# Delta rule decay exponents: one fp32 product against two float32r products

## The chip, the cores and the metric

The kernel is one program on one of the eight cores of a Trainium2 chip. The metric is the device time of one execution in microseconds. A core has TensorE (PE, matrix products; its weight loads are told apart as PEld), VectorE (DVE), ScalarE (ACT), GpSimd (POOL) and SyncE (SP), which issues most of the transfers. Each works through a queue of its own in the order in which the program was built; semaphores make one engine wait for another. Nothing is reordered on the chip, so that an instruction that waits holds up all that is queued behind it on its engine.

## What is computed

Two transformer blocks run one after the other on 256 tokens of width 1024, everything in fp32 to the outside. The first is attention, cross attention to a memory and a feed-forward part. The change lies in the second, a hybrid layer: one projection of the normalized input gives the inputs of a gated delta rule (8 heads), of a sparse attention with an indexer, and of two sigmoid gates that mix the two results; then come an output projection and a feed-forward part.

```
proj = rms_norm(x) @ w_in             # split into g_qkv, g_z, g_a, g_b, a_q, ..., gate_a, gate_b
g = -exp(a_log) * softplus(g_a + dt_bias)            # log decay, 8 heads
o_gdn = gated_delta_rule_chunked(gq, gk, gv, g, beta)
o_att = dsa_sparse_attention(...)
x = x + (sigmoid(gate_a) * norm(o_gdn) * silu(z) + sigmoid(gate_b) * o_att) @ w_out
x = x + square(relu(rms_norm(x) @ w_mlp_up)) @ w_mlp_down

# inside the delta rule, chunk by chunk:
g_cum = cumsum(g)
diff  = g_cum[:, None] - g_cum[None, :]
decay = where(incl, exp(diff), 0)                    # incl: lower triangle with diagonal
a_mat = where(strict, (k * beta) @ k.T * decay, 0)
u, w  = triangular_solve(I + a_mat, ...)
qk    = where(incl, q @ k.T * decay, 0)
```

The change is in how `diff` is formed. The kernel works in two chunks of 128 tokens. For each chunk and head it needs the 128x128 matrix of the sums of `g` from one token to another, and takes its exponential.

## The kernel before, in words

**Matrix products.** Nearly all large products are done in three float32r passes. A weight tile arrives as `raw` (128x1024 fp32), ScalarE casts it to its high half `whi`, and VectorE subtracts to get the low half `wlo`. The activations are split in the same way into `xhi` and `xlo` while they are transposed. `mm3` (line 233) then issues high x high, high x low and low x high into one PSUM bank. Small products with exact needs are fp32, and one fp32 product is two records in the trace.

**Emission.** The order of every queue is fixed when the program is built. The large products (the main stream) are emitted one after the other. After each third pass the builder calls `tick` (line 261), which lets side chains advance: generators such as `chain_gates`, `chain_decay`, the attention `dsa`, the delta rule `gdn`, and the gating at the end. A chain yields what it waits for, and `tick` resumes it once the builder's own running estimate of the engines' times (a fixed part and a rate for each engine, lines 113 to 120; `mm`, line 211, for TensorE) says that it is ready and that ScalarE and VectorE are not too far behind. `pump` (line 316) emits the next weight splits whenever a weight unit has been used. `finish` (line 272) drives given chains to their end. So each instruction that is emitted moves the estimate, and a later choice may come out another way.

**Around the change.** `consts2` (line 1060) builds the constants of block 2 in the course of block 1, among them `strict`, the strictly triangular matrix of zeros and ones; `tri` is the other triangle. `chain_gates` (line 1174) makes the log decays `gg` (128 x 2 chunks x 8 heads). `chain_decay(b)` (line 1338) runs for two halves of the heads and two chunks each: VectorE multiplies `tri` by the columns of `gg` into `gt` (four heads side by side, 128x512), TensorE adds up `strict` times `gt` and, with `identb` and `umb` in bf16, a large negative number above the diagonal, and ScalarE writes the exponential of the bank `ep` into `QE`. `chain_u` waits for it. Its results go into the triangular inverse (whose blocks are merged through `T` and `xp`), and further into the delta rule.

**The end of block 2.** The main stream ends with the products of the two gates: `gn`, for one gate, `gs` for its second half. Beside them run the last chains: attention scores, softmax rows `p`, their transposes on TensorE (`tb<-ident,p`, line 225), attention products `ao`, division by the row sums (`oat`), gating (`Z`), and the transposes of `Z` (`tb<-ident,Z`) whose split halves `xhi`, `xlo` are the input of the output projection, again `gs` products. `k.finish(*s_ga[0])` (line 1778) stands between gate and output projection. Then come a norm (`xg`) and the feed-forward part.

Of the kernel before, what the change touches and what calls it, by code (L numbers as in the profile page):

```python
# [9 lines left out]
F32 = mybir.dt.float32  # L10
F32R = mybir.dt.float32r
BF16 = mybir.dt.bfloat16
AF = mybir.ActivationFunctionType
OP = mybir.AluOpType
AX = mybir.AxisListType

P = 128
# [10 lines left out]
def bcast_rows(ap, n, parts=P):  # L28
    return bass.AP(tensor=ap.tensor, offset=ap.offset, ap=[[0, parts], [1, n]])


def rows(src, r0, nkt, c0, nc_):

    n = src.shape[1]
    return bass.AP(tensor=src.tensor, offset=src.offset + r0 * n + c0,
                   ap=[[n, P], [P * n, nkt], [1, nc_]])
# [6 lines left out]
def flat(ap):  # L43
    return ap.rearrange("p a b -> p (a b)")


def bc(ap, n):

    return ap[:, :, None].to_broadcast([P, ap.shape[1], n])


def mid(ap, n):

    return ap[:, None, :].to_broadcast([P, n, ap.shape[1]])
# [291 lines left out]
def split(k, hi, lo, src, scale=None):  # L346
    nc = k.nc
    if scale is None:
        nc.scalar.copy(hi, src)
        nc.vector.tensor_tensor(lo, src, hi.bitcast(F32), op=OP.subtract)  # L350
    else:
        nc.scalar.activation(hi, src, AF.Copy, scale=scale)
        nc.vector.scalar_tensor_tensor(lo, src, scale, hi.bitcast(F32), op0=OP.mult, op1=OP.subtract)
# [305 lines left out]
def join(sides):  # L659

    if sides:
        yield list(sides)
# [397 lines left out]
def consts2(k, w_in, conv_t, a_log, dt_bias, gdn_norm_g, q_norm_g, k_norm_g, rope_tab):  # L1060

    nc = k.nc
    dma = nc.sync.dma_start

    yield 30.0
    raw = k.t4([P, KT, 88], name="w88")
    dma(raw[:, :, 0:16], rows(w_in, 0, KT, C_AB, 16))
    yield 8.0
    dma(raw[:, :, 16:88], rows(w_in, 0, KT, C_IK, 72))
    yield 12.0  # L1070
    k.rt = k.keep([P, 2, 96], "rt")
    dma(k.rt, rope_tab.rearrange("(h p) c -> p h c", p=P))
    k.cw = k.keep([P, 24, 4], "cw")
    yield 8.0
    dma(k.cw, conv_t)
    yield 5.0
    k.dtb, k.nal = k.keep([P, 8], "dtb"), k.keep([P, 8], "nal")
    dma(k.dtb, bcast_rows(dt_bias, 8))
    dma(k.nal, bcast_rows(a_log, 8))
    yield 5.0  # L1080
    qkg = k.t2([P, 2, P], name="qkg")
    dma(qkg[:, 0], bcast_rows(q_norm_g, P))
    dma(qkg[:, 1], bcast_rows(k_norm_g, P))
    yield 5.0
    k.gng = k.keep([P, P], "gng")
    dma(k.gng, bcast_rows(gdn_norm_g, P))
    yield raw, k.gng
    k.w88 = k.t4([P, KT, 88], F32R, "w88h"), k.t4([P, KT, 88], F32R, "w88l")
    split(k, k.w88[0], k.w88[1], raw)
    yield qkg  # L1090

    k.rg = [k.keep([P, 2, 64], f"rg{i}") for i in range(2)]
    for i in range(2):
        for h in range(2):
            g = qkg[:, i]
            nc.vector.tensor_tensor(k.rg[i][:, h, 0:32], k.rt[:, h, 0:32], g[:, 0:32], op=OP.mult)
            nc.vector.tensor_tensor(k.rg[i][:, h, 32:48], k.rt[:, h, 32:48], g[:, 16:32], op=OP.mult)
            nc.vector.tensor_tensor(k.rg[i][:, h, 48:64], k.rt[:, h, 48:64], g[:, 0:16], op=OP.mult)
    k.gqk = k.keep([P, P], "gqk")
    nc.vector.memset(k.gqk[:, 0:32], 1.0)  # L1100
    nc.vector.tensor_tensor(k.gqk[:, 32:], qkg[:, 0, 32:], qkg[:, 1, 32:], op=OP.mult)

    k.strict = k.keep([P, P], "strict")
    nc.gpsimd.affine_select(k.strict, k.ones, pattern=[[-1, P]], compare_op=OP.is_gt, fill=0.0,
                            base=0, channel_multiplier=1)
    um = k.t2([P, P], name="um")
    nc.gpsimd.memset(um, 0.0)
    nc.gpsimd.affine_select(um, um, pattern=[[1, P]], compare_op=OP.is_ge, fill=NEG,
                            base=0, channel_multiplier=-1)
    k.umb = k.keep([P, P], "umb", BF16)  # L1110
    nc.gpsimd.tensor_copy(k.umb, um)

    k.bm = k.keep([P, 4], "bm")
    nc.gpsimd.affine_select(k.bm, k.ones[:, :4], pattern=[[-32, 4]], compare_op=OP.is_ge, fill=0.0,
                            base=0, channel_multiplier=1)
    nc.gpsimd.affine_select(k.bm, k.bm, pattern=[[32, 4]], compare_op=OP.is_gt, fill=0.0,
                            base=32, channel_multiplier=-1)

    k.bt = k.keep([P, 2], "bt")
    nc.gpsimd.tensor_tensor(k.bt[:, 0:1], k.bm[:, 0:1], k.bm[:, 2:3], op=OP.add)  # L1120
    nc.gpsimd.tensor_copy(k.bt[:, 1:2], k.bm[:, 1:2])
# [18 lines left out]
def block2(k, x3, ht, st, out, conv_w, norm_mlp_g):  # L1140
    nc = k.nc
# [27 lines left out]
    s_small = k.add(chain_small())  # L1169


    gx, ge, gg, beta, iw = (k.keep([P, 2, 8], n) for n in ("gx", "ge", "gg", "beta", "iw"))

    def chain_gates():
        yield from join([s_small])
        yield sml
        nc.vector.tensor_tensor(gx, sml[:, :, 0:8], mid(k.dtb, 2), op=OP.add)
        nc.scalar.activation(beta, sml[:, :, 8:16], AF.Exp, scale=-1.0)
        nc.vector.scalar_tensor_tensor(ge, gx, -1.0, gx, op0=OP.mult, op1=OP.min)
        nc.scalar.activation(ge, ge, AF.Exp)  # L1180
        nc.scalar.activation(k.nal, k.nal, AF.Exp)
        nc.scalar.activation(ge, ge, AF.Ln, bias=1.0)
        yield ge
        nc.vector.scalar_tensor_tensor(gx, gx, 0.0, ge, op0=OP.max, op1=OP.add)
        nc.vector.scalar_tensor_tensor(gg, gx, -1.0, mid(k.nal, 2), op0=OP.mult, op1=OP.mult)
        nc.vector.tensor_scalar(beta, beta, 1.0, None, op0=OP.add)
        nc.vector.reciprocal(beta, beta)
    s_gates = k.add(chain_gates())


# [129 lines left out]
    tri = k.tri1[:, :P]  # L1320
# [17 lines left out]
    def chain_decay(b):  # L1338

        yield from join([s_gates])  # L1340
        yield gg
        for ch in range(2):
            gt = k.t2([P, 4, P], name="gt")
            nc.vector.tensor_tensor(gt, mid(tri, 4), bc(gg[:, ch, 4 * b:4 * b + 4], P), op=OP.mult)
            yield gt
            ep = yield from k.get((P, 4, P), "ep")
            k.mm(flat(ep), k.strict, flat(gt), True, False)
            k.mm(ep, k.identb, mid(k.umb, 4), False, True)
            yield ep
            nc.scalar.activation(QE[ch][:, 4 * b:4 * b + 4], ep, AF.Exp)  # L1350
            k.put()
# [33 lines left out]

    s_dec = k.add(chain_dec())
    s_decay = [k.add(chain_decay(b)) for b in range(2)]
    s_u = []
    gemm_t(k, ht, D, conv_evac(kc, 8, lambda b, sides: s_u.append(k.add(chain_u(b, sides), rank=0))))
# [416 lines left out]
@with_exitstack  # L1806
def tile_kernel(ctx, tc, x, mem, w_in, b_fgt, rel, g_fox_out, g_chk_out, w_out, g_mix_pre, g_mix_post,
                g_mem_kv, w_mq, w_mk, w_mv, w_mo, g_mem_pre, g_mem_post, w_ff1, w_ff2, g_ff_pre, g_ff_post,
                norm_mix_g_2, w_in_2, conv_t, a_log_2, dt_bias_2, gdn_norm_g_2, q_norm_g_2, k_norm_g_2,
                w_out_2, norm_mlp_g_2, w_mlp_up_2, w_mlp_down_2, rope_tab, out):  # L1810
    k = Kern(ctx, tc)
    ctx.enter_context(tc.manual_schedule())
    k.units = units1(w_in, w_mk, w_mv, w_out, w_mq, w_mo, w_ff1, w_ff2)
    k.units += units2(w_in_2, w_out_2, w_mlp_up_2, w_mlp_down_2)
    box = []

    def xt_next():
        if not box:
            box.append(XT(k))
        return box[0]  # L1820
    x3, st = block1(k, x, mem, w_in, b_fgt, rel, g_fox_out, g_chk_out, w_out, g_mix_pre, g_mix_post,
                    g_mem_kv, w_mq, w_mk, w_mv, w_mo, g_mem_pre, g_mem_post, w_ff1, w_ff2, g_ff_pre, g_ff_post,
                    norm_mix_g_2, xt_next,
                    lambda: k.add(consts2(k, w_in_2, conv_t, a_log_2, dt_bias_2, gdn_norm_g_2, q_norm_g_2,
                                          k_norm_g_2, rope_tab)))
    block2(k, x3, box[0], st, out, conv_t, norm_mlp_g_2)
    k.finish()
# [53 lines left out]
```

## Time and profile before

| | |
|---|---|
| three runs | 885.59, 886.88 and 889.85 us; median 886.88 |
| the profiled execution | 885.71 us, span 883.7 |
| TensorE busy | 873.8 us, 99% of the span, 5704 matmul records |
| VectorE busy | 589.5 us, 67% |
| ScalarE busy | 455.2 us, 52% |
| GpSimd busy | 90.0 us, 10% |

A timeline row gives the start of an instruction or of a group of like ones, its duration, the engine, the line, out<-in, the size, and in brackets how long the engine had been idle before it and whose result it waited for. Line 96 is the helper through which all instructions of ScalarE, VectorE and GpSimd pass, line 212 the helper for products and 225 that for transposes; so work is told apart by the names of its tiles. Records of matrix products overlap, since they are pipelined: two rows at 0.23 us distance can each show 0.39 us.

### The profile page before, as it was taken

How to read it: one execution, taken by the hardware profiler on the slowest of the kernel's cores; microseconds unless marked ns; L12 is line 12 of the kernel's file. 1: busy time of each engine (PE TensorE's matmuls, PEld its weight loads, DVE VectorE, ACT ScalarE, POOL GpSimd, SP SyncE). 2: the span in 40 equal slices, each digit the busy share in tenths (PEclk: the TensorE clock that was granted, in tenths of full speed). 3: DMA queues.
4: the chain of work that ended last, by engine and by line, in shares of the span. 5: the costliest groups of instructions: out<-in, count | busy, mean ns of one | idle time of the engine just before them, and what ended most of it. 6: DMA issues, size and time to landing. Idle time of an engine off the chain costs nothing.

```text
span 883.7 us, 14576 instructions
## 1 busy us (share of the span) xinstructions
PE 873.8 (99%) x5704; PEld 774.7 (88%) x5704; DVE 589.5 (67%) x1028; ACT 455.2 (52%) x779; POOL 90.0 (10%) x150
## 2 busy tenths in 40 slices
PE   8999999999999999999999999999999999999998
PEld 7979998899789999998798899988987889999997
DVE  5675665765687556554769999979578875555541
ACT  6674654554475444442656665554564654444440
POOL 3101010100020000000100038800010000000000
PEclk9999999999999999999999999999999999999999
DMA  8992437383377766654651677395125586666521
GB/s 266 293 253 73 144 121 254 104 263 112 90 245 223 203 197 183 189 187 154 172 152 49 191 173 199 82 251 168 49 74 193 179 247 211 192 187 185 195 80 48
DMA packets 162615, 150.86 MB, mean 171 GB/s; under 512 B 20082, under 2 KB 127218, under 8 KB 162547
## 3 DMA queue, kind: packets, MB, share of 16 engines
q1 hardware_dynamic: 161970, 148.88, 56.6%
q10 hardware_dynamic: 576, 1.05, 0.4%
q8 instruction: 45, 0.74, 0.3%
q14 instruction: 24, 0.19, 0.1%
HBM read 148.08 MB, written 1.84 MB: 170 GB/s over the span
## 4 chain that ended last, share of the span: by engine, by line
PE 92%; DVE 4%; ACT 3%; issue 0%; DMA 0%; POOL 0%; DVEq 0%; ACTq 0%; POOLq 0%
PE gt L212 33%; PE acc L212 20%; PE gs L212 13%; PE gn L212 11%; PE tb L225 3%; PE mo L212 3%; DVE wlo L96 1%; PE o L212 1%; ACT p L96 1%; ACT whi L96 1%; PE ops L212 1%; PE ms L212 1%; PE s L212 1%; ACT junk L96 1%; DVE Z L96 1%; PE qp L212 1%
## 5 line engine op out<-in xcount | busy, mean ns | idle before, releaser
L96 DVE TENSOR_TENSOR wlo<-raw,whi 128x1024 fp32r<-128x1024 f32 (+1 forms) x263 | 315.1, 1225 | 111.8 <-ACT whi L96 110.2
L96 ACT CAST whi<-raw 128x1024 fp32r<-128x1024 f32 (+1 forms) x264 | 268.1, 1047 | 85.7 <-DMA raw<-in_w_in_dram 32.3
L212 PE MATMUL gt<-xhi,whi 128*128 128x256 f32 x832 | 239.0, 287 | 0.0
L212 PE MATMUL gt<-xlo,whi 128*128 128x256 f32 x832 | 233.7, 281 | 0.0
L212 PE MATMUL gt<-xhi,wlo 128*128 128x256 f32 x832 | 233.4, 281 | 0.0
L212 PEld LDWEIGHTS gt<-xhi,whi 128*128 128x128 f32 x832 | 156.9, 189 | 1.9 <-issue 1.3
L212 PEld LDWEIGHTS gt<-xlo,whi 128*128 128x128 f32 x832 | 156.9, 189 | 0.6
L212 PEld LDWEIGHTS gt<-xhi,wlo 128*128 128x128 f32 x832 | 156.9, 189 | 0.0
L212 PE MATMUL acc<-whi,ul 128*128 128x512 f32 (+1 forms) x288 | 106.1, 369 | 0.0
L212 PE MATMUL acc<-wlo,uh 128*128 128x512 f32 (+1 forms) x288 | 106.1, 369 | 0.0
L212 PE MATMUL acc<-whi,uh 128*128 128x512 f32 (+1 forms) x288 | 106.1, 368 | 0.0
L212 PE MATMUL gs<-whi,xhi 128*128 128x512 f32 (+1 forms) x208 | 80.6, 388 | 0.5 <-ACT xhi L96 0.5
L212 PE MATMUL gs<-whi,xlo 128*128 128x512 f32 (+1 forms) x208 | 79.1, 380 | 0.3 <-DVE xlo L96 0.3
L212 PE MATMUL gs<-wlo,xhi 128*128 128x512 f32 (+1 forms) x208 | 78.8, 379 | 0.1
L212 PE MATMUL gn<-whi,xhi 128*128 128x512 f32 x160 | 67.3, 420 | 0.0
L212 PE MATMUL gn<-whi,xlo 128*128 128x512 f32 x160 | 63.0, 394 | 0.0
L212 PE MATMUL gn<-wlo,xhi 128*128 128x512 f32 x160 | 62.8, 393 | 0.0
L212 PEld LDWEIGHTS acc<-whi,ul 128*128 128x128 f32 x288 | 54.1, 188 | 9.7
L212 PEld LDWEIGHTS acc<-whi,uh 128*128 128x128 f32 x288 | 54.1, 188 | 9.6
L212 PEld LDWEIGHTS acc<-wlo,uh 128*128 128x128 f32 x288 | 54.2, 188 | 9.5
L96 DVE TENSOR_TENSOR r<-r 128x512 f32<-128x512 f32 x32 | 22.1, 690 | 59.9 <-ACT r L96 59.9
L96 ACT ACTIVATE r<-gt 128x512 f32<-128x512 f32 x24 | 14.3, 598 | 76.1 <-PE gt L212 76.1
(364 smaller groups left out, 1129.2 us busy)
## 6 DMA issues: line engine op xcount, KB each, us to landing
raw<-in_w_in_dram SPq DMA_DIRECT2D x84, 512.0 KB, 4.8
raw<-in_w_ff_dram SPq DMA_DIRECT2D x64, 512.0 KB, 4.7
raw<-in_w_mlp_up_dram SPq DMA_DIRECT2D x32, 512.0 KB, 5.8
raw<-in_w_mlp_down_dram SPq DMA_DIRECT2D x32, 512.0 KB, 4.4
raw<-in_w_out_dram SPq DMA_DIRECT2D x16, 512.0 KB, 4.1
raw<-in_w_mk_dram SPq DMA_DIRECT2D x8, 512.0 KB, 4.1
raw<-in_w_mv_dram SPq DMA_DIRECT2D x8, 512.0 KB, 4.1
raw<-in_w_mq_dram SPq DMA_DIRECT2D x8, 512.0 KB, 4.5
```

The costliest lines, as they stand in the source:

```text
L96: f(*args, **kw)
L212: self.nc.tensor.matmul(out, lhsT, rhs, start=start, stop=stop)
L225: self.nc.tensor.transpose(out, in_, self.ident[:n, :n])
```

## The change

The log decays `gg` are split into a high part `ggh`, rounded to float32r by a ScalarE copy, and the rest `ggl`, subtracted on VectorE. Matrices of both are made: the high one, `gth`, on ScalarE as four scaled copies of `tri` of 128x128, the low one, `gtl`, on VectorE in the place of `gt`. Since `strict` holds only zeros and ones, its copy `strictr` in float32r is exact, and two float32r passes take the place of the fp32 product. The chain now waits for `ggl` where it waited for `gg`, and for `gth` and `gtl` where it waited for `gt`.

```
--- before.py
+++ after.py
@@ -1103,6 +1103,8 @@
     k.strict = k.keep([P, P], "strict")
     nc.gpsimd.affine_select(k.strict, k.ones, pattern=[[-1, P]], compare_op=OP.is_gt, fill=0.0,
                             base=0, channel_multiplier=1)
+    k.strictr = k.keep([P, P], "strictr", F32R)
+    nc.scalar.copy(k.strictr, k.strict)
     um = k.t2([P, P], name="um")
     nc.gpsimd.memset(um, 0.0)
     nc.gpsimd.affine_select(um, um, pattern=[[1, P]], compare_op=OP.is_ge, fill=NEG,
@@ -1169,7 +1171,8 @@
     s_small = k.add(chain_small())
 
 
-    gx, ge, gg, beta, iw = (k.keep([P, 2, 8], n) for n in ("gx", "ge", "gg", "beta", "iw"))
+    gx, ge, gg, beta, iw, ggl = (k.keep([P, 2, 8], n) for n in ("gx", "ge", "gg", "beta", "iw", "ggl"))
+    ggh = k.keep([P, 2, 8], "ggh", F32R)
 
     def chain_gates():
         yield from join([s_small])
@@ -1183,8 +1186,10 @@
         yield ge
         nc.vector.scalar_tensor_tensor(gx, gx, 0.0, ge, op0=OP.max, op1=OP.add)
         nc.vector.scalar_tensor_tensor(gg, gx, -1.0, mid(k.nal, 2), op0=OP.mult, op1=OP.mult)
+        nc.scalar.copy(ggh, gg)
         nc.vector.tensor_scalar(beta, beta, 1.0, None, op0=OP.add)
         nc.vector.reciprocal(beta, beta)
+        nc.vector.tensor_tensor(ggl, gg, ggh.bitcast(F32), op=OP.subtract)
     s_gates = k.add(chain_gates())
 
 
@@ -1338,13 +1343,17 @@
     def chain_decay(b):
 
         yield from join([s_gates])
-        yield gg
+        yield ggl
         for ch in range(2):
-            gt = k.t2([P, 4, P], name="gt")
-            nc.vector.tensor_tensor(gt, mid(tri, 4), bc(gg[:, ch, 4 * b:4 * b + 4], P), op=OP.mult)
-            yield gt
+
+            gh, gl = (k.t2([P, 4, P], F32R, n) for n in ("gth", "gtl"))
+            for j in range(4):
+                nc.scalar.activation(gh[:, j], tri, AF.Copy, scale=ggh[:, ch, 4 * b + j:4 * b + j + 1].bitcast(F32))
+            nc.vector.tensor_tensor(gl, mid(tri, 4), bc(ggl[:, ch, 4 * b:4 * b + 4], P), op=OP.mult)
+            yield gh, gl
             ep = yield from k.get((P, 4, P), "ep")
-            k.mm(flat(ep), k.strict, flat(gt), True, False)
+            k.mm(flat(ep), k.strictr, flat(gh), True, False)
+            k.mm(flat(ep), k.strictr, flat(gl), False, False)
             k.mm(ep, k.identb, mid(k.umb, 4), False, True)
             yield ep
             nc.scalar.activation(QE[ch][:, 4 * b:4 * b + 4], ep, AF.Exp)
```

TensorE's queue gets `ep<-gth,strictr` and `ep<-gtl,strictr` where `ep<-gt,strict` stood, four times; apart from that, all engines issue the same work as before. But the new instructions move the builder's estimate, and from the beginning of `chain_gates` to the start of the feed-forward part many of them stand in another place. Three places follow, each the difference of the two orders: - is the row before, + the row now.

VectorE, after the last softmax scaling `nmx`: `Z` here is the attention-free part of the merged tile, scaled by head (four products of 128x128 for each half of the tokens), `wlo` a weight split.

```order
 L96 TENSOR_TENSOR nmx<-mx,nasc 128x2
-L96 TENSOR_TENSOR t_7026<-t_7026,r_7025 128x4
-L96 SCALAR_TENSOR_TENSOR Z<-qs__6855,t_7026,Z 128x128 x4
-L96 TENSOR_TENSOR wlo<-raw,whi 128x1024
-L96 TENSOR_TENSOR t_7063<-t_7063,r_7062 128x4
-L96 SCALAR_TENSOR_TENSOR Z<-qs__6857,t_7063,Z 128x128 x4
-L96 TENSOR_TENSOR wlo<-raw,whi 128x1024
+L96 TENSOR_TENSOR wlo<-raw,whi 128x1024
+L96 TENSOR_TENSOR t_7077<-t_7077,r_7076 128x4
+L96 SCALAR_TENSOR_TENSOR Z<-qs__6895,t_7077,Z 128x128 x4
+L96 TENSOR_TENSOR t_7095<-t_7095,r_7094 128x4
+L96 SCALAR_TENSOR_TENSOR Z<-qs__6897,t_7095,Z 128x128 x4
```

One split that stood between and one that stood behind the two groups of `Z` are gone there, and one now stands ahead of both. The other stands further up, ahead of the scores.

VectorE, where the gate has been applied and the output projection begins: `Z<-gt__7183` and its successor are the third merged tile, `xlo` the low half of the transposed tiles.

```order
-L96 SCALAR_TENSOR_TENSOR Z<-gt__7183,Z 128x512
+L96 SCALAR_TENSOR_TENSOR Z<-gt__7205,Z 128x512
 L96 TENSOR_TENSOR Z<-Z,oat 128x512
-L96 TENSOR_TENSOR wlo<-raw,whi 128x1024 x2
-L96 SCALAR_TENSOR_TENSOR xlo<-tb,xhi 128x4x128
-L96 TENSOR_TENSOR wlo<-raw,whi 128x1024
+L96 TENSOR_TENSOR wlo<-raw,whi 128x1024 x3
 L96 SCALAR_TENSOR_TENSOR xlo<-tb,xhi 128x4x128 x2
 L96 TENSOR_TENSOR wlo<-raw,whi 128x1024 x4
```

Three weight splits now stand in a row ahead of the first `xlo`, where two stood; the fourth stands behind two `xlo`.

TensorE at the end of the gate product: `tb` are transposes of merged tiles, the `gs` rows ahead of them belong to the gate product, those behind them to the output projection.

```order
 L212 MATMUL gs<-wlo,xhi 128x512
 L212 MATMUL gs<-whi,xlo 128x512
-L212 MATMUL gs<-whi,xhi 128x512
-L212 MATMUL gs<-wlo,xhi 128x512
-L212 MATMUL gs<-whi,xlo 128x512
+L225 MATMUL tb<-ident,Z 128x128 x8
 L212 MATMUL gs<-whi,xhi 128x512
 L212 MATMUL gs<-wlo,xhi 128x512
```

Before, the gate product had the transposes of the first tile nine products ahead of its end, those of the second three ahead, and those of the third at its end. Now those of the first and the third stand together at its end, and those of the second follow three products of the output projection later.

Counted in the whole orders, in products of 512 columns: the last-but-one group of `ao` was followed by 15 gate products, three transposes of `p`, and 9 more gate products up to the last `ao`; it is now followed by 18, the transposes, and 6. Behind the last `ao` stood 45 products of the gate, now 30. The whole attention group stands 15 products later against the main stream, the merge products `xp` 12 products earlier, and the transposes of the second norm 12 products earlier.

## Rows read from the trace of the kernel before

**Rows 1.** Page, first part: each engine's busy us, share of the span, instructions.
```profile
PE 873.8 (99%) x5704; PEld 774.7 (88%) x5704; DVE 589.5 (67%) x1028; ACT 455.2 (52%) x779; POOL 90.0 (10%) x150
```

**Rows 2.** Waits of TensorE: engine, operation, producer waited for; us in total, times, longest.
```profile
PE tb L225 <- ACT p L96: 0.8, 4, 0.3
...
PE gs L212 <- ACT xhi L96: 0.5, 2, 0.3
...
PE gs L212 <- DVE xlo L96: 0.3, 1, 0.3
```

**Rows 3.** Timeline of PE, 653 to 662: start us, us, instruction, count, [idle before].
```profile
655.34 0.48 PE L212 MATMUL gn<-whi,xhi 128*128 128x512 f32 x1
655.66 0.39 PE L212 MATMUL gn<-wlo,xhi 128*128 128x512 f32 x1
655.89 0.40 PE L212 MATMUL gn<-whi,xlo 128*128 128x512 f32 x1
```

**Rows 4.** Timeline of PE, 672 to 677: output projection begins.
```profile
674.32 0.39 PE L212 MATMUL gs<-wlo,xhi 128*128 128x512 f32 x1
675.05 0.50 PE L212 MATMUL gs<-whi,xlo 128*128 128x512 f32 x1 [0.35 <-DVE xlo L96]
```

**Rows 5.** Timeline of PE, 460 to 480: the decay exponents.
```profile
468.54 1.12 PE L212 MATMUL ep<-gt,strict 128*128 128x512 f32 x2
469.50 0.38 PE L212 MATMUL ep<-umb,identb 128*128 128x512 bf16 x1
469.71 1.02 PE L212 MATMUL ep<-gt,strict 128*128 128x512 f32 x2
470.57 0.38 PE L212 MATMUL ep<-umb,identb 128*128 128x512 bf16 x1
```

**Rows 6.** Timeline of ACT, 455 to 481: a scaled copy of 256 columns.
```profile
460.44 0.84 ACT L96 ACTIVATE cy<-gt,cw 128x256 f32<-128x256 f32 x2 [1.55 <-PE gt L212]
```

**Rows 7.** Windows: stretch, its us, busy us of PE, PEld, DVE, ACT, POOL; clock, DMA.
```profile
460.00:480.00 20.00, 20.00 (x149) 16.20 (x148) 19.02 (x56) 13.86 (x29) 0.00 (x0) 1.00 0.19 54
```

**Rows 8.** Timeline of PE, 600 to 675: transposes of the softmax rows.
```profile
618.25 0.49 PE L225 MATMUL tb<-ident,p 128*128 128x128 f32 x3
...
647.11 0.29 PE L225 MATMUL tb<-ident,p 128*128 128x128 f32 x1
647.66 0.44 PE L225 MATMUL tb<-ident,p 128*128 128x128 f32 x2 [0.26 <-ACT p L96]
```

**Rows 9.** Timeline of DVE, 655 to 675: the chain to the output projection.
```profile
657.83 0.16 DVE L96 TENSOR_TENSOR nmx<-mx,nasc 128x2 f32<-128x2 f32 x1
...
661.38 0.15 DVE L96 TENSOR_TENSOR t<-t,r 128x4 f32<-128x4 f32 x1
...
662.75 1.23 DVE L96 TENSOR_TENSOR wlo<-raw,whi 128x1024 fp32r<-128x1024 f32 x1
663.90 0.17 DVE L96 RECIPROCAL ars<-asum 128x4 f32<-128x4 f32 x1
...
671.43 0.69 DVE L96 TENSOR_TENSOR Z<-Z,oat 128x512 f32<-128x512 f32 x1
672.04 2.35 DVE L96 TENSOR_TENSOR wlo<-raw,whi 128x1024 fp32r<-128x1024 f32 x2
674.31 0.68 DVE L96 SCALAR_TENSOR_TENSOR xlo<-tb,xhi 128x512 fp32r<-128x512 f32 x1
```

**Rows 10.** Timeline of ACT, 655 to 662: between scores and gate.
```profile
658.09 0.49 ACT L96 ACTIVATE p<-lg,nmx,asc 128x128 f32<-128x128 f32 x1 [1.53 <-DVE t L96]
...
659.17 1.03 ACT L96 CAST whi<-raw 128x1024 fp32r<-128x1024 f32 x1
660.10 0.59 ACT L96 ACTIVATE gt__7123<-gn 128x512 f32<-128x512 f32 x1
```

**Rows 11.** Tile T: operations, duration ns min/median/max, first and last start.
```profile
L212 PE MATMUL xp<-T,U x96: 190/191/267, 598.4 to 610.0; 32*32 32x32 f32 x64, 64*64 64x64 f32 x32
...
L96 ACT ACTIVATE T<-tpk,bt x2: 732/748/764, 590.1 to 590.7; 128x512 f32<-128x512 f32 x2
```

More of the change, by code (lines that the diff above doesn't have):

```diff
@@ L1105, in consts2 @@
                             base=0, channel_multiplier=1)
+    k.strictr = k.keep([P, P], "strictr", F32R)
+    nc.scalar.copy(k.strictr, k.strict)
     um = k.t2([P, P], name="um")
@@ L1169, in block2 @@
     s_small = k.add(chain_small())
-    gx, ge, gg, beta, iw = (k.keep([P, 2, 8], n) for n in ("gx", "ge", "gg", "beta", "iw"))
+    gx, ge, gg, beta, iw, ggl = (k.keep([P, 2, 8], n) for n in ("gx", "ge", "gg", "beta", "iw", "ggl"))
+    ggh = k.keep([P, 2, 8], "ggh", F32R)
     def chain_gates():
@@ L1185, in chain_gates @@
         nc.vector.scalar_tensor_tensor(gg, gx, -1.0, mid(k.nal, 2), op0=OP.mult, op1=OP.mult)
+        nc.scalar.copy(ggh, gg)
         nc.vector.tensor_scalar(beta, beta, 1.0, None, op0=OP.add)
         nc.vector.reciprocal(beta, beta)
+        nc.vector.tensor_tensor(ggl, gg, ggh.bitcast(F32), op=OP.subtract)
     s_gates = k.add(chain_gates())
@@ L1340, in chain_decay @@
         yield from join([s_gates])
-        yield gg
+        yield ggl
         for ch in range(2):
-            gt = k.t2([P, 4, P], name="gt")
-            nc.vector.tensor_tensor(gt, mid(tri, 4), bc(gg[:, ch, 4 * b:4 * b + 4], P), op=OP.mult)
-            yield gt
+            gh, gl = (k.t2([P, 4, P], F32R, n) for n in ("gth", "gtl"))
+            for j in range(4):
+                nc.scalar.activation(gh[:, j], tri, AF.Copy, scale=ggh[:, ch, 4 * b + j:4 * b + j + 1].bitcast(F32))
+            nc.vector.tensor_tensor(gl, mid(tri, 4), bc(ggl[:, ch, 4 * b:4 * b + 4], P), op=OP.mult)
+            yield gh, gl
             ep = yield from k.get((P, 4, P), "ep")
-            k.mm(flat(ep), k.strict, flat(gt), True, False)
+            k.mm(flat(ep), k.strictr, flat(gh), True, False)
+            k.mm(flat(ep), k.strictr, flat(gl), False, False)
             k.mm(ep, k.identb, mid(k.umb, 4), False, True)
```

## The prediction

> **What bounds the kernel now.** I read the page's first part, then the list of what TensorE waited for, then timelines of single engines at the two places where the new program differs in a way that could matter. TensorE is busy 99% of the span [rows 1], and its waits on a named producer in the second block are tiny: 0.8 us in four waits for the softmax rows `p`, 0.5 in two for the activations' high half `xhi`, 0.3 for one low half `xlo` [rows 2]. A busy matmul record overlaps its neighbour, so I take the pace from start to start. In an undisturbed run of gate products the starts stand 0.23 us apart (655.66 to 655.89), the one after a switch from fp32 takes 0.32 [rows 3]. So the kernel is TensorE's queue, one product after the other, and an edit counts if it changes what that queue holds or makes it stand still. The second is possible where a long dependent chain (attention, delta rule, gating, output projection) must end before the queue can go on. The last such place is around 675 us: the first output product with `xlo` starts at 675.05, 0.73 us after its predecessor, where 0.23 is the pace [rows 4].
>
> **The products themselves.** The change touches four fp32 products `ep<-gt,strict`, each two records. Read start to start in [rows 5], the first takes 0.96 us (468.54 to 469.50), the second 0.86 (469.71 to 470.57); the other two read like the second, so 0.96 + 3 x 0.86 = 3.5 us. In their place come eight float32r products of 128x512. No float32r product on `strictr` is in the trace; the nearest rows are the gate products, float32r of the same width, at 0.23 us: 8 x 0.23 = 1.8 us. Gain 1.7 us. The other end is that a pass costs what an fp32 record costs, 0.43 us: 8 x 0.43 = 3.5, gain nothing. I take 1.7, the row of the same type and width. The Trainium skill (TensorE: Matmul & The Clock Gate, "Back-to-back issue gap") gives about 131 ns for a 512-column product in a stream of loads and products; this trace does not agree, its row says 230 ns. By the page the gain would be about 2.5 us, an estimate from that page.
>
> **ScalarE and VectorE around them.** ScalarE gets sixteen 128x128 scaled copies, and three small casts. The nearest row is a scaled copy of 256 columns, two in 0.84 us [rows 6], so one copy costs between half of 0.42 and all of it: 3.4 to 6.7 us in sum. ScalarE is busy 13.9 of 20 us between 460 and 480 and TensorE does not stand still there [rows 7], and the copies are issued some 45 products of 256 columns ahead of the first `ep`: I cost them at nothing. If that cover is gone, the excess over the 6.1 idle us stalls TensorE, 0.6 us at most. VectorE makes the four low matrices in place of four of the same size, and one 16-column subtraction: it stays at 19 of 20 us busy, and loses below 0.2 us. That is hidden too, since TensorE does not wait for a weight split here. `strictr` is one copy, far ahead in block 1: nothing.
>
> **The order.** The builder lets side chains run by its own running estimate of engine times, and the new instructions shift every decision after 460 us. Counted in the whole orders of before and of the change, the last-but-one group of attention products (`ao`, which ends at 655.34 when the gate product `gn` resumes [rows 3]) now stands 15 products of 512 columns later in TensorE's queue: 15 x 0.23 = 3.5 us. All that comes before it is otherwise the same work. Ahead of it two waits of TensorE inside the transposes of `p` should go: a group of three takes 0.49 us undisturbed, 0.99 at 647.11 and about as much in the group after it [rows 8], 1.0 us too much in sum; they have six more gate products between scores and transposes now. So that point comes at 3.5 - 1.7 - 1.0 = +0.8 us. The bounds: 0.8 if both gains come, 3.5 if neither.
>
> From that point on TensorE has less left to do before it must have the merged activations. The last `ao` used to be followed by 45 gate products, now by 30. The chain from 655.34 is VectorE's, and its length doesn't shrink with that. Before: softmax scaling `nmx` at 657.83, attention output scaled from 663.90, third merged tile `Z` done at 672.12 (671.43 + 0.69), two weight splits `wlo` until 674.31, `xlo` until 674.99 [rows 9], and TensorE at 675.05 [rows 4]: 19.7 us. Now: after `nmx` (+2.65) ScalarE does `p`, a gate tanh and the cast `whi`; these take 1.08 (658.09 to 659.17), 0.5 and 0.95 us [rows 10], so +5.2; the split `wlo`, 1.13, now stands ahead of the `Z` products, then two groups of four products with their small scaling, 1.37 each (661.38 to 662.75), which gives +9.1 where it was 8.56. The third `Z` follows 8.2 us later as before (663.90 to 672.12), +17.3. Then three splits stand ahead of `xlo` instead of two: 3 x 1.13 = 3.4, so `xlo` begins at +20.7 and ends at +21.4, against 19.65: 1.7 us more. `nmx` itself may come 0.7 earlier, since one split less stands ahead of it while the chain waits; I take +1.2, with 0.3 (the splits find idle time) and 3.4 (all three add) as ends.
>
> TensorE meets this at two spots. The transposes of the first and the third `Z` now stand together, right behind the gate product; the second of them waits about 2 us for its `Z`. Then the third output product waits about 3 us for `xlo`. Before, the same stretch held 0.5 us. After the output projection the block's second norm has its transposes 12 products earlier than before, but one split less ahead of them on VectorE, so I cost it at nothing; if it isn't covered, below 1 us. The rest (feed-forward) is the same order.
>
> **Sum:** 3.5 (15 products moved ahead) - 1.7 (passes) - 1.0 (waits gone) + 1.2 (longer chain) = +2.0 us. The profiled execution took 885.71 us, so 887.7. It lies 1.2 us below the median of the three runs, 886.88; from the median it would be 888.9. I forecast 888.2, between. With all lower ends the sum is 3.5 - 1.7 - 1.0 + 0.3 = +1.1, with all upper ends 3.5 + 3.4 = +6.9.
>
> **Rivals.** (1) The chain is no limit, TensorE's shorter queue shows in full: 885.7 - 1.7 - 1.0 = 883.0. For it: 99% busy, waits of 1.6 us in the list [rows 1, 2]. Against it: in [rows 4, 9] the chain ended right at TensorE's need, and it now starts later in the queue; it needs `Z` and `xlo` some 4 us sooner than my count. The Trainium skill (Perfetto Trace Analysis, "Identifying Performance Opportunities") says that a kernel generally improves with its most-contended engine, which here is TensorE; that would be this rival, and the trace bears it out for the long gemm stretches only.
> (2) Slower than 0.5%: a new wait further up, at the merge of the inverse blocks. Its first product `xp` starts at 598.4 and its input `T` is written from 590.1 on, by 591.5 [rows 11]. In the new queue it stands 12 products earlier, 2.8 us, and the passes give 1.7: TensorE comes at 593.9, with 2.4 us of slack left instead of 6.9. `T` hangs on GpSimd and two DMAs, which don't get faster with TensorE. If `T` comes more than 2.4 us later relative to now, TensorE stands still for the excess, and it decides once it eats the 2.7 us of gains: 885.7 + 3.5 + 1.2 = 890.4, and 1:1 more beyond. Against it: the products that feed `T` stand 9 earlier too.
> (3) The change doesn't do what it says: a float32r pass on these operands is no faster than an fp32 record. The order moves all the same: +3.7, 889.4.
>
> **How the numbers follow.** Forecast 0.62 (886.8 to 890), rival 1 0.18, rival 2 0.13, rival 3 0.07. About 0.5% (4.4 us) is what a measurement of this kernel can tell from no change. Faster than 882.4 only rival 1 with luck in the runs reaches: 0.06. Slower than 891.3 needs rival 2 with a large wait or the upper ends together: 0.12. Same 0.82. The range goes from 883.0 (rival 1) to 891.5 (the lower part of rival 2, and the scatter of the runs).
>
> **What would show it.** Right: `ep` products at about 0.23 us start to start; no wait inside the transposes of `p` before the last `ao`; a wait of TensorE of some 2 us before a `tb<-Z` and of some 3 before a `gs` product with `xlo`, where three `wlo` precede `xlo` on VectorE; the first output product with `xlo` at about 677. Wrong: these two waits below 1 us in sum, or a wait before `xp` or `ep`, or `ep` at 0.43.

## The result

| | before | changed |
|---|---|---|
| median of the runs | 887.05 us (6 runs, 885.59 to 889.91) | 894.80 us (6 runs, 893.66 to 894.96) |
| ratio | | 1.0084, 95% interval 1.0069 to 1.0098 |
| profiled execution, span | 885.71, 883.7 us | 894.82, 893.1 us |

The change makes the kernel 0.84% slower, 7.8 us between the medians and 9.1 us between the two profiled executions. The prediction was 888.2 us with 883.0 to 891.5 around it: the sign of its sum was right, the size was not, and the time lies outside the range.

### The profile page after: what moved, and what is told of

Its sections match the earlier page's. It is cut to its first block, busy times and chain, and to the rows that moved or that the text cites. A ratio compares the mean times of both kernels' runs of the same rounds, so it can differ in the third digit from the quotient of the medians.

```text
span 893.1 us, 14596 instructions
## 1 busy us (share of the span) xinstructions
PE 876.6 (98%) x5704; PEld 775.4 (87%) x5704; DVE 590.9 (66%) x1029; ACT 461.1 (52%) x797; POOL 88.7 (10%) x150
## 4 chain that ended last, share of the span: by engine, by line
PE 90%; DVE 5%; ACT 4%; issue 1%; DMA 0%; POOL 0%; DVEq 0%; ACTq 0%; POOLq 0%
PE gt L212 32%; PE acc L212 20%; PE gs L212 13%; PE gn L212 11%; PE tb L225 3%; PE mo L212 3%; DVE wlo L96 2%; PE o L212 1%; ACT p L96 1%; ACT whi L96 1%; DVE Z L96 1%; PE ops L212 1%; PE ms L212 1%; PE s L212 1%; ACT junk L96 1%
```

## The profile after

First the page: the busy times, which answer to [rows 1], and the clock granted to TensorE in 40 slices.

```profile
PE 876.6 (98%) x5704; PEld 775.4 (87%) x5704; DVE 590.9 (66%) x1029; ACT 461.1 (52%) x797; POOL 88.7 (10%) x150
...
PEclk9999999999999999999999999999997999999999
```

TensorE is busy 2.8 us longer with the same 5704 records, and stands still 6.6 us more (the span is 9.4 longer). In one slice (670 to 692 us) the clock is below 9 tenths. Then TensorE's waits (us in total, times, longest), which answer to [rows 2].

```profile
PE tb L225 <- DVE Z L96: 3.0, 2, 2.0
PE gs L212 <- DVE xlo L96: 2.0, 1, 2.0
PE s L212 <- DVE oat L96: 0.8, 1, 0.8
PE ao L212 <- ACT pt L96: 0.8, 1, 0.8
...
PE tb L225 <- ACT p L96: 0.4, 2, 0.3
```

Five of the 9 us stand in the first two lines, where before there were 0.3 us in sum. The waits for `oat` and `pt` are new as well; of the transposes of `p` 0.4 us are left of 0.8 (0.2 of each lie in block 1).

The products of the change themselves, one of four pairs in TensorE's timeline (start us, us, instruction), answer to [rows 5].

```profile
471.02 0.58 PE L212 MATMUL ep<-gth,strictr 128*128 128x512 f32 x1
471.44 0.40 PE L212 MATMUL ep<-gtl,strictr 128*128 128x512 f32 x1
471.68 0.39 PE L212 MATMUL ep<-umb,identb 128*128 128x512 bf16 x1
```

This pair and its switch take 0.66 us (471.02 to 471.68), where the fp32 product took 0.86; the others take 0.56, 0.47 and 0.66. Over all four it is 2.36 us instead of 3.54, 1.2 us gained.

Next the point which the prediction calls the last-but-one `ao` group; it answers to [rows 3].

```profile
659.47 0.94 PE L212 MATMUL ao<-kv,pt 128*128 128x128 f32 x6 [0.75 <-ACT pt L96]
660.16 0.48 PE L212 MATMUL gn<-whi,xhi 128*128 128x512 f32 x1
```

It ends at 660.16, where it was 655.34: 4.8 us later, of which 0.3 us lie ahead of all changes (from 276 to 455 us the second program runs 0.3 us behind the first). TensorE's timeline from there to the output projection answers to [rows 4].

```profile
673.55 0.40 PE L212 MATMUL gs<-whi,xlo 128*128 128x512 f32 x1
674.93 0.66 PE L225 MATMUL tb<-ident,Z 128*128 128x128 f32 x4 [0.99 <-DVE Z L96]
677.59 1.11 PE L225 MATMUL tb<-ident,Z 128*128 128x128 f32 x4 [2.00 <-DVE Z L96]
...
681.60 0.79 PE L212 MATMUL gs<-whi,xlo 128*128 128x512 f32 x1 [2.04 <-DVE xlo L96]
682.19 1.05 PE L225 MATMUL tb<-ident,Z 128*128 128x128 f32 x4
682.90 0.77 PE L212 MATMUL gs<-whi,xhi 128*128 128x512 f32 x1
683.47 0.63 PE L212 MATMUL gs<-wlo,xhi 128*128 128x512 f32 x1
683.90 0.63 PE L212 MATMUL gs<-whi,xlo 128*128 128x512 f32 x1
...
686.75 0.39 PE L212 MATMUL gs<-whi,xhi 128*128 128x512 f32 x1
```

The last pass of the gate product starts at 673.55, TensorE waits 1.0 us for the first `Z` and 2.0 us for the third, then 2.0 us for `xlo`. What follows, from 682.90 on, are the same products as before, but 0.43 us apart in place of 0.23 (683.47 to 683.90), until 686.75. VectorE in the same stretch, as in [rows 9]:

```profile
662.77 0.16 DVE L96 TENSOR_TENSOR nmx<-mx,nasc 128x2 f32<-128x2 f32 x1
...
676.85 0.69 DVE L96 TENSOR_TENSOR Z<-Z,oat 128x512 f32<-128x512 f32 x1
677.46 3.49 DVE L96 TENSOR_TENSOR wlo<-raw,whi 128x1024 fp32r<-128x1024 f32 x3
680.86 1.29 DVE L96 SCALAR_TENSOR_TENSOR xlo<-tb,xhi 128x512 fp32r<-128x512 f32 x2
```

Three `wlo` stand from 677.46 to 680.86, and `xlo` after them. Last the windows of that stretch: us, busy us of PE, PEld, DVE, ACT, POOL, granted clock, DMA share, GB/s.

```profile
673.80:675.00 1.20, 0.21 (x2) 0.07 (x2) 1.17 (x3) 0.60 (x1) 0.00 (x0) 1.00 0.00 0
...
676.00:677.00 1.00, 0.00 (x0) 0.00 (x0) 0.97 (x3) 0.23 (x1) 0.00 (x0) 0.67 0.00 0
...
682.00:686.00 4.00, 4.00 (x12) 3.17 (x12) 2.50 (x3) 1.87 (x2) 0.00 (x0) 0.50 0.89 286
...
687.00:690.00 3.00, 3.00 (x15) 2.44 (x14) 2.30 (x4) 1.55 (x3) 0.00 (x0) 1.00 1.02 378
```

The clock is full in the first stretch, falls while TensorE stands still in the second, and is at a half (1.2 of 2.4 GHz) over the four microseconds from 682 to 686, in which TensorE is busy without a break. At 687 it is full again. The Trainium skill (TensorE: Matmul & The Clock Gate, "What's actually happening") says that the array runs at half its clock after it has stood idle, and comes back to the full one only after it has been busy for a while; the rows agree: 0.67 at 676 to 677, where no product runs, 0.50 at 682 to 686, with PE busy 4.00 of 4.00, and 1.00 at 687.

So the 9.3 us at 686.75 (the tenth product behind the one that waited for `xlo`, 677.47 before) are: 0.3 from ahead of the change, 4.5 until the `ao` group, 1.7 more in the chain from there (660.16 to 681.60 is 21.4 us, 655.34 to 675.05 was 19.7), 2.3 of products at half the clock (681.60 to 686.75 is 5.15 us; ten products at 0.23 and four transposes with their switches, 0.54, make 2.85), and 0.45 for the second tile's transposes, which used to stand ahead of the wait.

## The experiments

Two theories. **Order:** the time went into where instructions now stand (TensorE reaches the output projection with too little left to do, waits, and loses its clock). **Arithmetic:** the added copies, matrices or float32r passes themselves cost it. Times of the kernel before are those of the same chip and session, 886.4 to 886.7 us. TensorE's 5704 records stand in one order in the kernel before and e1, in one in the changed kernel and e2, and in one in e10 and e13.

**e1: the changed arithmetic in the old order.** The new instructions are issued without the builder's estimate being told of them (`eng` is the engine itself, behind the helper of line 96 that keeps the estimate; the gates' two instructions and `strictr` go the same way):

```
-        nc.scalar.copy(ggh, gg)
+        nc.scalar.eng.copy(ggh, gg)
-                nc.scalar.activation(gh[:, j], tri, ...)
+                nc.scalar.eng.activation(gh[:, j], tri, ...)
-            k.mm(flat(ep), k.strictr, flat(gh), True, False)
-            k.mm(flat(ep), k.strictr, flat(gl), False, False)
+            k.nc.tensor.matmul(flat(ep), k.strictr, flat(gh), start=True, stop=False)
+            k.nc.tensor.matmul(flat(ep), k.strictr, flat(gl), start=False, stop=False)
+            k.clock = max(k.clock, k.ready(k.strict, gl)) + 4 * P * 4 / 2400
```

> The changed arithmetic (high and low matrices, two float32r passes), but every queue in the order of the kernel before: the added instructions don't move the builder's estimate. Theory (the loss is the new order: waits of TensorE and the clock that falls in them): the passes take 2.36 us where they took 3.54, so 1.2 us below the kernel before, about 885.9 against 887.05, granted clock 1.00, no wait before the transposes of Z. Rival (the added copies on ScalarE or the float32r passes themselves cost the time): at least half of the loss stays, 891 or more.

Measured: 887.34 us (11 runs) against 886.42, ratio 1.0010 (1.0002 to 1.0019). The rival's 891 is out, most of the loss is gone with the old order. But the 1.2 us were not gained either: 0.9 us were lost. TensorE's timeline shows two waits that the kernel before did not have there:

```profile
469.02 0.71 PE L212 MATMUL lp<-ikT,iqT 64*128 64x128 f32 x8 [1.03 <-ACT iqT L96]
...
478.08 0.50 PE L1355 MATMUL ep<-gth,strictr 128*128 128x512 f32 x1 [0.97 <-ACT rl L96]
```

and ScalarE's shows what stands ahead of `iqT`, for which the first of them waits (e1, then the kernel before):

```profile
463.16 2.46 ACT L1351 ACTIVATE gth<-tri,ggh 128x128 fp32r<-128x128 f32 x8
...
468.35 0.62 ACT L96 COPY iqT<-tb 128x512 f32<-128x512 f32 x1
```

```profile
466.63 0.58 ACT L96 COPY iqT<-tb 128x512 f32<-128x512 f32 x1 [2.06 <-PE tb L225]
```

The eight copies take 2.4 us, and `iqT` starts at 468.35, where it was 466.63. So the cover at which I costed the copies at nothing does not hold in this order: the two waits cost 2.0 us, more than the 1.2 that the passes bring.

**e2: the old arithmetic in the new order.** The reverse: the estimate is told of instructions that are not issued.

```
+            for j in range(4):
+                k.note("act", [gh[:, j]], [tri, ggh], 0.09 + P * 0.00084)
-            k.mm(flat(ep), k.strict, flat(gt), True, False)
+            k.nc.tensor.matmul(flat(ep), k.strict, flat(gl), start=True, stop=False)
+            k.clock = max(k.clock, k.ready(gh)) + 4 * P / 2400
+            k.clock = max(k.clock, k.ready(gl)) + 4 * P / 2400
```

> The old arithmetic (one fp32 product), but every queue in the order of the changed kernel: the builder's estimate is told of instructions that are not issued. Theory (order): 894.8 plus the 1.2 us of the passes, some 896, with the waits before tb<-Z and before the gs product with xlo and the granted clock below 1 between 660 and 700. Rival (arithmetic): within 2 us of the kernel before, 887.

Measured: 895.41 us against 886.42, ratio 1.0100 (1.0087 to 1.0113), with the same waits (3.0 us before `tb<-Z` in two, 2.5 before `gs` with `xlo`) and a mean clock of 0.91 between 660 and 700. No instruction of the change is in it. The order alone costs 9.0 us; the changed kernel, with the same order and its passes, costs 7.8 over its own comparison. These 1.2 us less are no bigger than the uncertainty of the two ratios. The traces show 1.0 up to the first tile's transposes (the first `ep` at 470.42 and 470.48, `tb<-Z` at 674.93 and 676.00), and only 0.3 in the span, since in e2 the clock comes back sooner (ten products and four transposes behind the wait for `xlo` take 4.42 us, in the changed kernel 5.15).

**e3: the waits filled.** Products into a bank that the next product overwrites keep TensorE busy in its waits:

```
+def fillers(k, ps, n):
+    for _ in range(n):
+        k.nc.tensor.matmul(ps, k.identb, mid(k.umb, 4), start=True, stop=True)
 def transposes(k, srcs, n=P, fill=0):
     ps = yield from k.get((P, 4, P), "tb")
+    fillers(k, ps, fill)          # 3 and 7 for the first and the third tile
...
+                    fillers(k, ps[0], 7)      # ahead of the first output product
```

> The changed kernel with products that nobody reads in TensorE's waits: 3 of 512 columns in bf16 ahead of the first tile's transposes, 7 ahead of the third tile's, 7 ahead of the first output product (all into a bank that the next product overwrites). Theory (of the loss, 2.3 us are products at the lower of the two clocks after the waits, the rest the chain on VectorE): the granted clock stays at 1.00, the third output product starts at about the same 681.6, what follows runs at 0.23 instead of 0.43 us, so 892.5. Rival (the clock does not fall because TensorE stands idle there, or the slow products are hidden by another chain): 894.8 or, with the fillers in the way, more.

Measured: 892.39 us (892.08 to 893.56), 2.4 us below the changed kernel, and a clock of 1.00 throughout; waits of 0.3, 0.5 and 1.4 us stay. TensorE's timeline:

```profile
677.72 1.67 PE L448 MATMUL gs<-umb,identb 128*128 128x512 bf16 x7
...
681.23 0.51 PE L212 MATMUL gs<-whi,xlo 128*128 128x512 f32 x1 [1.37 <-DVE xlo L96]
...
682.24 0.39 PE L212 MATMUL gs<-wlo,xhi 128*128 128x512 f32 x1
682.47 0.40 PE L212 MATMUL gs<-whi,xlo 128*128 128x512 f32 x1
```

The third output product starts at 681.23 (681.60 in the changed kernel, which was 0.36 us behind at the first tile's transposes already), and what follows is 0.23 us apart. The ten products and four transposes behind it take 2.86 us, in the changed kernel 5.15: 2.3 us, as reckoned. The medians give 2.4 us, the two ratios to the kernel before (1.0084 and 1.0069) 1.3 with an uncertainty as large. So that the clock falls because TensorE stands still is shown by this; its price is shown by the rows, and the times alone would not prove it.

**e4: the splits behind `xlo`.** `pump` does nothing between the second half of the gate product and the end of the first tiles:

```
     def pump(self):
+        if self.defer:
+            return
...
-    gemm_n_skew(k, ht, 1, ...)
+    gemm_n_skew(k, ht, 1, ..., before_b=lambda: setattr(k, "defer", True))
     k.finish(*s_ga[0])
+    k.defer = False
```

> The changed kernel, but the three weight splits ahead of the first xlo are issued behind it (casts and subtractions both). Theory (the second wait is those splits): xlo follows its xhi (678.74 + 0.6) at about 680.0 instead of 681.5, so 1.5 us off, and up to 1 us more if the clock comes back sooner: 892.3 to 893.3. Rival (the output projection then lacks weights, since transfers wait for splits to free their buffers): a wait for raw or wlo in its place, 894.8 or more.

Measured: 892.92 us (892.60 to 894.43), inside the theory's 892.3 to 893.3. TensorE's timeline:

```profile
677.23 0.66 PE L225 MATMUL tb<-ident,Z 128*128 128x128 f32 x4 [2.00 <-DVE Z L96]
...
678.19 0.55 PE L212 MATMUL gs<-whi,xlo 128*128 128x512 f32 x1
...
680.25 0.63 PE L212 MATMUL gs<-whi,xlo 128*128 128x512 f32 x1
680.67 0.63 PE L212 MATMUL gs<-whi,xhi 128*128 128x512 f32 x1
```

and VectorE's:

```profile
677.09 0.69 DVE L96 SCALAR_TENSOR_TENSOR xlo<-tb,xhi 128x512 fp32r<-128x512 f32 x1
```

The wait for `xlo` is gone and the third output product starts at 678.19, 3.4 us earlier and not 1.5: the `xlo` that it needs is the first tile's, whose `xhi` starts at 675.63 in the changed kernel, and not the one behind the `xhi` of 678.74 that the expectation took. So `xlo` can run right behind the third `Z`. The clock still falls, only later (0.43 us apart from 679.82 to 681.52), and new waits, 0.8 us for a `wlo` at 689.48 and 0.5 us for the fourth tile's `Z` at 692.83, give a part back. The edit also moves what follows (the fourth tile's transposes stand 6 products later), so the total is not the place of the splits alone. It lies inside the theory's range by luck; what e4 shows is the wait that went.

**e8: both together,** the edit of e4 and that of e3 without the fillers ahead of the output product:

```
-                    fillers(k, ps[0], 7)
```

> The changed kernel with both of the earlier edits: splits behind the first xlo (as in e4), and fillers of 3 and 7 products ahead of the first and the third tile's transposes (as in e3, none ahead of the output product). Theory (the slow clock and the splits are separate terms): third output product at about 678.2 as in e4, but the products behind it at 0.23 us instead of 0.43, so 1.6 us below e4's 892.9: 891.2. Rival (something behind the drain, weights or the norm, sets the end): 892.4 or more.

Measured: 894.09 us (892.78 to 896.48), and not 891.2: the theory that the two terms add is wrong. The clock is 1.00, but TensorE now waits for weights:

```profile
PE gs L212 <- DVE wlo L96: 2.0, 3, 0.8
...
PE gs L212 <- ACT whi L96: 0.5, 1, 0.5
```

Of these 2.5 us the kernel e4 had 0.8. With the splits put off and the products at full pace, the output projection overtakes its weights; the slow clock of e4 had stood where this wait stands now. It is longer than e4 by 1.2 us in the medians; its runs scatter over 3.7 us, and of the 1.5 us between the two profiled spans 0.8 lie ahead of all that differs (`dp<-gg` at 464.19 and 463.39). The rest stays open.

**e7: the high matrices on GpSimd,** old order, one multiplication of 128x512 for four copies:

```
-            for j in range(4):
-                nc.scalar.eng.activation(gh[:, j], tri, ...)
+            nc.gpsimd.eng.tensor_tensor(gh, mid(tri, 4), bc(ggh[:, ch, 4 * b:4 * b + 4], P), op=OP.mult)
```

> As e1 (changed arithmetic, old order), but GpSimd makes each high matrix in one multiplication of 128x512 in place of four scaled copies on ScalarE. Theory (e1 lost its 1.2 us because the sixteen copies, 0.3 us each, push iqT and rl back in ScalarE's queue, for which TensorE then waits): these waits go, 1.2 us below the kernel before, about 885.2 against 886.4. Rival (the loss in e1 comes with the passes, or GpSimd is too slow: a wait before ep on gth): 887.3 or more.

Measured: 887.99 us against 886.42, ratio 1.0024 (1.0013 to 1.0034). ScalarE is free now (`iqT` at 467.47), and yet nothing is won. GpSimd's timeline, VectorE's, and VectorE's in the kernel before (the profiled execution of e7, 891.91 us, was the longest of twelve; only durations are read from it):

```profile
463.28 2.09 POOL L1350 TENSOR_TENSOR gth<-tri,ggh 128x512 fp32r<-128x512 f32 x2 [4.94 <-ACT ggh L1189]
470.20 2.68 POOL L1350 TENSOR_TENSOR gth<-tri,ggh 128x512 fp32r<-128x512 f32 x2 [4.83 <-PE ep L1355]
```

```profile
463.32 2.19 DVE L96 SCALAR_TENSOR_TENSOR kv<-kv,rsk,gqk 128x128 f32<-128x128 f32 x2
...
470.83 1.02 DVE L96 TENSOR_SCALAR negc<-dec 128x8 f32<-128x8 f32 x1
...
472.04 0.92 DVE L96 COPY sc<-mask 128x128 f32<-128x128 f32 x1
```

```profile
462.39 0.52 DVE L96 SCALAR_TENSOR_TENSOR kv<-kv,rsk,gqk 128x128 f32<-128x128 f32 x2
...
468.23 0.16 DVE L96 TENSOR_SCALAR negc<-dec 128x8 f32<-128x8 f32 x1
```

Two products on `kv` that took 0.52 us now take 2.19, from 463.32 on, one instruction of 8 columns takes 1.02 in place of 0.16, a copy 0.92 in place of 0.16, each until about the time when a multiplication of GpSimd beside it is over. VectorE's instructions last about as long as GpSimd works. The Trainium skill (SBUF — State Buffer, "Who interferes with whom") says that the two share one pair of ports, which one instruction holds to its end, and which a VectorE instruction needs for a second operand from SBUF or in a faster mode; the durations agree (2.19 us beside 2.09). On an engine busy 19 of 20 us [rows 7] that is late work for TensorE, here in waits for `cy`, `rl` and `vc`. My theory that ScalarE's queue alone had cost e1 its gain is therefore not confirmed by e7; what e7 shows is that GpSimd is no free engine here.

**e9, e11, e12: the attention earlier.** The estimate is told of the gates' two small instructions alone:

```
-        nc.scalar.eng.copy(ggh, gg)
+        nc.scalar.copy(ggh, gg)
-        nc.vector.eng.tensor_tensor(ggl, gg, ...)
+        nc.vector.tensor_tensor(ggl, gg, ...)
-        yield gg
+        yield ggl
```

The last attention products then stand 12 gate products earlier than before (the expectations say 13, a miscount). e9 makes the high matrices on GpSimd, e11 on ScalarE, e12 has the old fp32 products in the same order.

> As e7, but the builder's estimate is told of the two small instructions in the gates' chain alone; the last two attention groups then stand 13 products earlier than in the kernel before. Theory (what counts is the number of gate products left behind the attention): no wait at the end of the gate product, 0.5 us below e7, 884.7. Rival (the attention's own chain does not come earlier, TensorE waits for p, pt or oat by what it saved): equal to e7 or up to 3 us above it.

> As e9 (attention 13 products earlier), but the high matrices by sixteen copies on ScalarE, as in e1, in place of GpSimd. Theory (e9 still pays for VectorE standing still while GpSimd multiplies, 1.6 + 0.9 + 0.8 us of VectorE; the copies cost TensorE about as much through ScalarE's queue): 885.5 to 886.0, within 0.5 us of e9. Rival (one of the two engines is free there): 1 us or more apart.

> The order of e9 and e11 with the old fp32 products and nothing added on ScalarE or GpSimd. Theory (the gain of 1.2 us from the passes is eaten by what their matrices cost on ScalarE or VectorE): equal to e9 and e11 within 0.5 us, 885.7. Rival (the passes pay in a good order): 1.2 us above e9 and e11, 887.1.

Measured: e9 885.96 us, ratio 0.9996 (0.9986 to 1.0005); e11 886.02, 0.9999 (0.9990 to 1.0007); e12 885.79, 0.9993 (0.9983 to 1.0003). All three are level with the kernel before and with each other. The wait before the transposes of `Z` is in none of them, and e9 is 2.0 us below e7, where 0.5 was expected; that it should be below 885 was not borne out. e11 shows again what the copies do where the builder does not know of them; this is its longest wait of TensorE in the second block (us in total, times, longest), which e12 doesn't have:

```profile
PE lp L212 <- ACT iqT L96: 1.5, 1, 1.5
```

The passes' 1.2 us go into it. That the passes pay in a good order, the rival of e12, is not shown by these three; it takes an order that has room for the copies, as in e10 and e13.

**e10: the changed kernel with one estimate changed.** The builder's estimate for the four decay products is left at its old value. All other new instructions are known to it, but for the copy to `strictr` in block 1, which is issued as in e1; e13 tells the builder of that copy and comes out in the same order, so it plays no part:

```
-            k.mm(flat(ep), k.strictr, flat(gh), True, False)
-            k.mm(flat(ep), k.strictr, flat(gl), False, False)
+            k.nc.tensor.matmul(flat(ep), k.strictr, flat(gh), start=True, stop=False)
+            k.nc.tensor.matmul(flat(ep), k.strictr, flat(gl), start=False, stop=False)
+            k.clock = max(k.clock, k.ready(k.strict, gl)) + 4 * P * 4 / 2400
```

> The changed kernel in full, every new instruction known to the builder, but the builder's estimate of TensorE for the decay products is left at the fp32 cost, 0.85 us in place of 0.43 for each of four. Every queue comes out in another order again: the last attention products stand 51 gate products ahead of the first tile's transposes, where the changed kernel has 30 and the kernel before 36. Theory (the order decides, and of it the number of products behind the attention): no wait before the transposes of Z, clock 1.00, so the passes' 1.2 us are left: 885.2 against 886.4 of the kernel before. Rival (the change itself costs, in whatever order): 889 or more.

Measured: 884.95 us (11 runs) against 886.66, ratio 0.9983 (0.9974 to 0.9992). The same instructions as in the changed kernel, 9.9 us faster, and faster than both kernels. (Behind the last attention product and ahead of the first tile's transposes stand 48 gate products; the 51 in the expectation was a miscount.) TensorE at the first decay product and at the end of the gate product:

```profile
470.27 0.47 PE L1355 MATMUL ep<-gth,strictr 128*128 128x512 f32 x1
...
672.01 0.60 PE L225 MATMUL tb<-ident,Z 128*128 128x128 f32 x4
672.37 0.47 PE L212 MATMUL gs<-whi,xhi 128*128 128x512 f32 x1
```

The third tile's transposes start at 672.01 without a wait, and no product waits behind them.

**e13: the order of e10 with the old arithmetic,** by the edit of e2 with the fp32 estimate:

```
-            k.clock = max(k.clock, k.ready(gh)) + 4 * P / 2400
-            k.clock = max(k.clock, k.ready(gl)) + 4 * P / 2400
+            k.clock = max(k.clock, k.ready(k.strict, gl)) + 4 * P * 4 / 2400
```

> The order of e10, queue by queue, with the old fp32 products and without the added instructions. Theory (in an order in which ScalarE's copies are foreseen the passes pay their 1.2 us): 1.2 us above e10's 884.95, 886.1, level with the kernel before. Rival (all of e10's gain is its order): equal to e10 within 0.4 us.

Measured: 886.22 us against 886.58, ratio 0.9993 (0.9983 to 1.0003), 1.3 us above e10 in the medians; the two ratios alone leave 0.9 with an uncertainty as large. TensorE at the same two places as in e10:

```profile
470.84 1.02 PE L1355 MATMUL ep<-gtl,strict 128*128 128x512 f32 x2
...
673.77 0.60 PE L225 MATMUL tb<-ident,Z 128*128 128x128 f32 x4
```

From the first to the second it is 202.93 us, in e10 201.74: 1.2 us. Here the passes pay what the rows say.

## Why the prediction was wrong

What held. The place (the end of the gate product) and the mechanism (TensorE has less left to do, and waits first for `Z` and then for `xlo`) were those of the forecast; e2 shows that they come with the order alone. The chain from the `ao` group was worked out to `xlo` beginning after 20.7 us, and it began after 20.7 (660.16 to 680.86). Its pieces held as well (the division by the row sums begins after 9.1 us, the third `Z` ends after 17.4, as said). The waits were 3.0 and 2.0 us where some 2 and 3 were said. Of the signs named for being right two did not come: one wait inside the transposes of `p` stayed, and the first output product with `xlo` started at 681.60 and not at 677.

**The step that failed first is the arrival of the `ao` group,** "that point comes at 3.5 - 1.7 - 1.0 = +0.8 us". It came at +4.5, above its own upper bound of 3.5. The 3.5 us of order stand: the trace has 15 more gate products ahead of that point. The passes gave 1.2 and not 1.7: a pair takes 0.47 to 0.66 us with the switch from and to the bf16 product, not twice 0.23. Of the 1.0 us for waits inside the transposes of `p` only 0.3 went. And the new order brought waits of its own, which the sum did not have; read from start to start they cost 0.95 us for `oat`, 0.95 for `pt` and 0.6 at the first products on `kc`. Together: 3.5 - 1.2 - 0.3 + 0.95 + 0.95 + 0.6 = 4.5. I priced what the move takes away and not what it puts in its place, for the producers moved in their own queues, too: `oat` now stands behind a weight split on VectorE (643.04; before ahead of one, at 636.89), and the third `pt` behind eight `junk` activations on ScalarE (658.96), of which it stood ahead of the last four before. For every product up to that point the place of its producer in the new order should have been looked up, as it was for `T`.

**The second step that failed is the sum itself,** which took a wait to cost its length. The 5 us of waits cost 2.3 us more, because the clock fell in them and the products behind them ran at half the pace. e3 shows the cause, and the price in its rows. There was no such row in the trace before, where the clock is 1.00 over the span and the longest wait in that stretch 0.35 us [rows 4], but this step had forecast waits of 2 and 3 us in a row, far longer than any there, and should have asked for it as an upper end.

The chain term itself, +1.2, was 1.7, since what I took off for an earlier `nmx` did not come: `nmx` starts 2.6 us behind the `ao` group now (660.16 to 662.77), and did so after 2.5 before. The transposes of the second tile, 0.45 us, were moved behind the wait and counted nowhere. With 3.7 for the arrival, 2.3 for the clock, 0.5 for the chain and the 0.3 from ahead of the change, that is the way from +2.0 to +9.3 us. The range was too narrow even by the prediction's own terms: all its upper ends make +6.9, 892.6 from the profiled execution, and it ended at 891.5.

Rival 1 (TensorE's saving shows in full) has its answer in e10 and e13: 1.2 us, once the order lets it. Rival 2 (a wait for `T`) did not come: `xp` started at 595.1, 3.3 us earlier, without a wait. Rival 3 is out, a pass runs at the pace of the gate products apart from the switch.

That ScalarE's copies cost nothing held where the builder knows of them (the changed kernel against e2, 1.0 us in favour of the passes up to the first tile's transposes, and e10 against e13, 1.2), and not where they were pushed into an order made without them (e1, 0.9 us lost; e11 against e12, 0.2).

Shown are the order as the cause (e1, e2, e10), the clock's share (e3), and that the three splits ahead of `xlo` hold it back (e4). Not tried by itself is the 3.5 us of the 15 products; it is read from the order and the rows alone. TensorE's two queues first part close behind the new copy to `ggh`: the transposes of `ik` and `kv` stood ahead of `dp<-gg` (463.08) and now follow it (466.68). Why the builder decides so there stays open.

## What to carry to other kernels

Where a builder places work by estimates, an edit is two changes: what it computes and what it does to every later decision. Measure them apart (the new work in the old order, the old work in the new one) before judging either; here one was worth 1.2 us and the other 9.0, and one estimate of 0.4 us per product turned 894.8 into 885.0. And when a forecast holds a wait of TensorE far longer than any that the trace shows in that stretch, as here, put into its upper end what the products behind the wait lose at half the clock.

## What had not been expected of the hardware

Products that nobody reads, put into the waits of TensorE, kept its clock at 1.00 and took 2.3 us off the products behind (5.15 to 2.86 us, e3). A GpSimd multiplication of 128x512 (2.09 us for two that overlap) held up VectorE instructions beside it for nearly its whole length: 0.52 us became 2.19, 0.16 became 1.02 (e7).
